# A hybrid attention and convolution layer on one core: last keys' product padded to 128 rows, Silu and Sqrt on ScalarE, a third seven-product pair in the first output block, halved first pieces and later copies

## The chip, the core and the metric

The kernel runs on one core of a Trainium2 chip. The core has five engines that run side by side and wait for each other through semaphores: TensorE (PE; its weight loads are shown as PEld), VectorE (DVE), ScalarE (ACT), GpSimd (POOL) and SyncE (SP), which issues most DMAs. The metric is the device time of one launch in microseconds (us), as a median of several runs. Each engine works its instructions in the order in which they were written to it, so an instruction that waits holds up what stands behind it on its engine.

## The reference

One layer over 272 positions (16 meta tokens ahead of 256 tokens), width 4096, all in float32. Only the 256 tokens' rows are returned.

```python
h = rmsnorm(x, norm_g)
p = h @ w_in                      # 4096 x 16384
q, k, v, g_attn, b, c, h, z = split(p)   # eight parts of 2048
o = stick_breaking_attention(q, k, v)    # 16 heads of 128, strictly causal
o = group_rmsnorm(o * silu(g_attn), attn_norm_g)
y = b * short_conv(c * h, conv_w)        # three taps along the positions
y = group_rmsnorm(y * silu(z), conv_norm_g)
return rmsnorm(x + concat([o, y]) @ w_out, final_norm_g)
```

## The kernel before

**Precision and products.** Each operand of a large product is split in a high part (a rounding cast on ACT, L409) and a low part (the rest, a subtraction on DVE, L405, called a "low" here). A product is then three products on TensorE: high by low, high by high, low by high (L442 to L444 for blocks, L450 to L453 for projections). Weights come in pieces of 128 x 1024, 512 KB each, through five buffers named `raw`; the split parts go to rings of six, `wh` and `wl`.

**Stages.** The sixteen heads and sixteen channel groups are worked as eight groups of two each. For a group the input projection has two kinds of pieces. Blocks ("p", one for each of k, v, c and h of a unit, four pieces of eight row chunks) give outputs with channels on the partitions; a piece is 24 products of 272 or 258 columns. Pairs (two row chunks, pieces "A" and "B") give q, g_attn, b and z with tokens on the partitions, 512 columns a product. A pair needs two by two token halves and column halves, eight products, three passes each. A **seven-product pair** does the same as Strassen's scheme does, in seven products, and has pieces "A", "B", "T", "U": sums of the tokens' blocks are made once and kept (`sum`, `lent`, in the output stage `osum`), sums of the weights are made on DVE at each pair (L426, L429, L431). Group 0 takes plain pairs only, the others seven-product pairs only.

Behind the eight groups comes the output projection: four blocks of 1024 (the last 768) columns, g = 8 to 11, in the same way over sixteen pairs each, and a last strip of 256 columns (pieces "o"). `sevens(g)` lists the pairs that take seven products: two (9, 10) in block 8, six (8 to 13) in the others. `OUT_ORDERS` gives the order of the pairs in each block. Behind a block's last seven-product pair `out_sums` (L921) adds its four special sums into the residual rows, eight DVE operations and one ACT copy; behind the block's last pair `out_blocks` (L972) evicts the four plain ones, eight DVE operations, and begins their squares. The sums of mixed pairs 8 to 13 (`kept_sums`, L302) are made when a group's mixed rows come back from memory (pieces "m" and "k").

**Order.** One loop over the pieces (L1026) writes everything: it loads seven pieces ahead, writes the products of piece i, splits piece i + 4, and then runs the tasks due at i (`later`, `run_tasks`). Up to the last pair of group 0, `top[0]`, and in the last eight pieces the order on the engines is left to the compiler's scheduler; between them it is the written order (`manual_schedule`, L1033).

**Attention of a group**, during the next group's pairs: queries are transposed, `scores` (L748) makes the masked scores, `weights` (L773) the weights through Abs, Tanh, Ln, Relu, two scans and Exp, `trans` (L794) turns them by 32 x 32 blocks into `at` (128 rows) and `a3` (the last sixteen keys, 16 rows). `v_block` (L586) does the same for the values, in `vv` (128 rows) and `v3` (16 rows); its copies are `vcopies` (L596). `po_mm` (L806) multiplies them: four products of 128 rows and one of 16 (L812). Then `squares`, `norm` and `mix` write the mixed rows. `plan_group` (L853) places all this; for the last group, 7, there is no next group, and it falls into the first output block, counted in pieces behind `f`, the end of the group's pairs.

**Gate.** `silu` (L668) computes Sigmoid on ACT and multiplies on POOL; the factor of the norm is put right later through `rt`, `rt2` and `fac`.

**Start.** TensorE runs ten products of a tile of ones (`warm`, L149) while x and the weights of the first pieces are loaded. `prep_x` scales x and splits it. The first two pieces are loaded and split in halves (`parts`, L371).

**Tail.** The last strip runs all products of tokens 0 to 127 first, then `finish(0)`, then those of tokens 128 to 255, then `finish(1)`. `finish` (L986) takes the inverse root by nine small DVE operations, a guess by integer arithmetic and two corrections, scales the rows in five parts on DVE and ACT and stores each.

## Time and profile before

| | before |
|---|---|
| runs | 1781.87, 1779.18, 1779.79 us |
| median | 1779.79 us |
| the profiled execution | 1778.96 us, its span 1777.2 us |
| TensorE clock granted | 0.998 |
| HBM read and written | 395.37 and 13.63 MB, 230 GB/s over the span |
| products (matmul instructions) | 10926 |
| first product of the kernel proper, last product | 6.87 us, 1765.51 us |

Times in the rows are counted from the first instruction of the span. A row of a timeline gives the start, the duration, engine, line, operation, what it writes and reads, shapes and how many were merged ("x2"); in square brackets the idle time of the engine before it and what ended it. A product's duration contains its passage through the array, and the next begins before it ends: the time that a product takes from TensorE's stream is read from start to start. A row of a group gives the count, the busy time, the mean of one in ns and idle time before. A row of waits names who waited for whom, the total in us, how often, and the longest.

### The profile page before, as it was taken

How to read it: one execution, taken by the hardware profiler on the slowest of the kernel's cores; microseconds unless marked ns; L12 is line 12 of the kernel's file. 1: busy time of each engine (PE TensorE's matmuls, PEld its weight loads, DVE VectorE, ACT ScalarE, POOL GpSimd, SP SyncE). 2: the span in 40 equal slices, each digit the busy share in tenths (PEclk: the TensorE clock that was granted, in tenths of full speed). 3: DMA queues.
4: the chain of work that ended last, by engine and by line, in shares of the span. 5: the costliest groups of instructions: out<-in, count | busy, mean ns of one | idle time of the engine just before them, and what ended most of it. 6: DMA issues, size and time to landing. Idle time of an engine off the chain costs nothing.

```text
span 1777.2 us, 29833 instructions
## 1 busy us (share of the span) xinstructions
PE 1762.1 (99%) x10926; PEld 1601.6 (90%) x10926; DVE 1590.3 (89%) x1929; ACT 1233.1 (69%) x2089; POOL 151.0 (8%) x184
## 2 busy tenths in 40 slices
PE   9999999999999999999999999999999999999997
PEld 7899999999999999999999999999999988888897
DVE  6776898999999999999999999999999888989986
ACT  6755677677767776777678768776777785555553
POOL 2143110011001100010101010101010110000000
PEclk9999999999999999999999999999999999999999
DMA  8977666766676667666766676667666676676565
GB/s 316 323 238 249 226 214 216 259 214 226 218 251 219 225 226 245 215 230 222 250 215 228 213 257 215 225 218 245 213 231 226 228 236 233 231 233 213 196 224 191
DMA packets 120819, 410.96 MB, mean 231 GB/s; under 512 B 13536, under 2 KB 18784, under 8 KB 120672
## 3 DMA queue, kind: packets, MB, share of 16 engines
q1 hardware_dynamic: 116640, 405.38, 67.3%
q10 hardware_dynamic: 4032, 3.67, 0.6%
q8 instruction: 86, 1.41, 0.3%
q14 instruction: 61, 0.50, 0.1%
HBM read 395.37 MB, written 13.63 MB: 230 GB/s over the span
## 4 chain that ended last, share of the span: by engine, by line
PE 97%; DMA 1%; ACT 1%; DVE 0%; SPq 0%; issue 0%; POOL 0%; DVEq 0%; ACTq 0%
PE P L450 17%; PE P L453 17%; PE P L452 17%; PE mm L444 14%; PE mm L443 14%; PE mm L442 14%; PE mo L955 0%; PE mo L954 0%; PE mo L953 0%; PE z L755 0%; PE po L812 0%; DMA mixd<-mfh 0%; ACT wh L409 0%; DMA raw<-w 0%; PE z L754 0%; DVE wl L405 0%
## 5 line engine op out<-in xcount | busy, mean ns | idle before, releaser
L405 DVE TENSOR_TENSOR wl<-raw,wh 128x1024 fp32r<-128x1024 f32 (+3 forms) x780 | 862.2, 1135 | 77.9 <-ACT wh L409 72.2
L409 ACT CAST wh<-raw 128x1024 fp32r<-128x1024 f32 (+3 forms) x780 | 721.0, 965 | 278.0 <-PE mm L443 68.2
L442 PE MATMUL mm<-xs,wh 128*128 128x258 f32 (+1 forms) x2048 | 582.5, 284 | 0.4 <-ACT wh L409 0.4
L444 PE MATMUL mm<-xs,wl 128*128 128x258 f32 (+1 forms) x2048 | 581.7, 284 | 0.8 <-DVE wl L405 0.8
L443 PE MATMUL mm<-xs,wh 128*128 128x258 f32 (+1 forms) x2048 | 581.7, 284 | 0.0
L442 PEld LDWEIGHTS mm<-xs,wh 128*128 128x128 f32 x2048 | 385.5, 188 | 4.6 <-ACT wh L409 0.8
L443 PEld LDWEIGHTS mm<-xs,wh 128*128 128x128 f32 x2048 | 385.7, 188 | 3.7
L444 PEld LDWEIGHTS mm<-xs,wl 128*128 128x128 f32 x2048 | 385.7, 188 | 1.0 <-DVE wl L405 1.0
L409 ACT CAST wh<-t 128x1024 fp32r<-128x1024 f32 (+1 forms) x132 | 137.7, 1043 | 142.9 <-DVE t L426 123.9
L450 PE MATMUL P<-wh,xs 128*128 128x512 f32 x464 | 180.8, 390 | 1.2 <-ACT wh L409 1.2
L453 PE MATMUL P<-wl,xs 128*128 128x512 f32 x464 | 180.7, 390 | 0.2 <-DVE wl L405 0.2
L452 PE MATMUL P<-wh,xs 128*128 128x512 f32 x464 | 180.5, 389 | 0.0
L405 DVE TENSOR_TENSOR wl<-t,wh 128x1024 fp32r<-128x1024 f32 (+1 forms) x132 | 158.7, 1202 | 8.8 <-ACT wh L409 8.8
L426 DVE TENSOR_TENSOR t<-raw,raw 128x1024 f32<-128x1024 f32 (+1 forms) x132 | 164.9, 1250 | 0.0
L450 PE MATMUL P<-wh,mixl 128*128 128x512 f32 (+1 forms) x412 | 155.7, 378 | 0.0
L453 PE MATMUL P<-wl,mixh 128*128 128x512 f32 (+1 forms) x412 | 155.1, 376 | 0.0
L452 PE MATMUL P<-wh,mixh 128*128 128x512 f32 (+1 forms) x412 | 155.0, 376 | 0.0
L450 PE MATMUL P<-wh,lent 128*128 128x512 f32 x308 | 123.6, 401 | 0.0
L453 PE MATMUL P<-wl,lent 128*128 128x512 f32 x308 | 120.2, 390 | 0.0
L452 PE MATMUL P<-wh,lent 128*128 128x512 f32 x308 | 120.1, 390 | 0.0
L450 PEld LDWEIGHTS P<-wh,xs 128*128 128x128 f32 x464 | 87.1, 188 | 19.8 <-ACT wh L409 1.4
L453 PEld LDWEIGHTS P<-wl,xs 128*128 128x128 f32 x464 | 87.1, 188 | 19.3 <-DVE wl L405 1.1
(238 smaller groups left out, 2136.5 us busy)
## 6 DMA issues: line engine op xcount, KB each, us to landing
raw<-w SPq DMA_DIRECT2D x614, 512.0 KB, 4.5
lent<-sumd SPq DMA_DIRECT2D x77, 512.0 KB, 5.9
raw<-w SPq DMA_DIRECT2D x32, 384.0 KB, 3.8
sumd<-lent SPq DMA_DIRECT2D x11, 512.0 KB, 5.2
raw<-xin SPq DMA_DIRECT2D x8, 512.0 KB, 5.4
raw<-mixd SPq DMA_DIRECT2D x8, 512.0 KB, 4.6
xr<-xt SPq DMA_DIRECT2D x15, 272.0 KB, 4.9
res<-xin SPq DMA_DIRECT2D x12, 256.0 KB, 4.9
```

The costliest lines, as they stand in the source:

```text
L405: nc.vector.tensor_tensor(out=lo[:, c], in0=t[:, c], in1=h[:, c].bitcast(F32), op=ALU.subtract)
L409: nc.scalar.copy(out=h[:, c], in_=t[:, c])
L426: nc.vector.tensor_tensor(out=s[:, :2 * hw].rearrange("p (a b) -> p a b", a=2), in0=a[:, :2 * hw].rearrange("p (a b) -> p a b", a=2), in1= ...
L442: nc.tensor.matmul(out=o, lhsT=h, rhs=x[:, 0, s:], start=k == 0, stop=False)
L443: nc.tensor.matmul(out=o, lhsT=h, rhs=x[:, 1, s:], start=False, stop=False)
L444: nc.tensor.matmul(out=o, lhsT=lo, rhs=x[:, 0, s:], start=False, stop=k == KC - 1)
L450: nc.tensor.matmul(out=o, lhsT=a[1], rhs=h, start=key not in begun, stop=False)
L452: nc.tensor.matmul(out=o, lhsT=a[0], rhs=h, start=False, stop=False)
L453: nc.tensor.matmul(out=o, lhsT=a[0], rhs=lo, start=False, stop=last)
```

## The change

- `a3` and `v3` get 128 rows, of which 16 are filled as before and the others stay zero; the two `v3` are made once and cleared on POOL at the start.
- The gate is one Silu on ACT in place; the tile `sg` and the products on POOL go, with them `rt2`.
- Pair 11 of block 8 takes seven products too. Block 9 is worked in the order 0 1 2 3 4 8 5 9 ... in place of 0 1 2 3 8 4 9 5 ....
- The values' transposes and copies of head 15 come two and three pieces behind the end of group 7's pairs, in place of its fourteenth pair (`v_block`), in a buffer of another ring; several tasks of the last group come one piece later.
- One warm-up product less; a one-column copy on ACT as its first work; five pieces instead of two split in halves; in the first two pieces the products with the high weights come ahead of those with the low ones, in twos; the cast of the kept token sums waits until the next piece "B" is split.
- The written order holds from the first piece on.
- `finish` takes Sqrt on ACT, a reciprocal and one correction on DVE.

```diff
-WARM = 10
+WARM = 9
+PARTS = 5
...
-    (0, 1, 2, 3, 8, 4, 9, 5, 10, 6, 11, 7, 12, 14, 13, 15),
+    (0, 1, 2, 3, 4, 8, 5, 9, 6, 10, 7, 11, 12, 14, 13, 15),
...
-    return OUT_SJ[1:3] if g == GROUPS else OUT_SJ if g > GROUPS else SJ if g else ()
+    return (9, 10, 11) if g == GROUPS else OUT_SJ if g > GROUPS else SJ if g else ()
...
     nc.vector.memset(ones, 1.0 / P)
+    first = wk.tile([P, P], F32, tag="junk", name="first")[:, :1]
+    nc.scalar.copy(out=first, in_=ones[:, :1])
...
-    a3 = const.tile([META, P], F32, name="a3")
+    a3 = const.tile([P, P], F32, name="a3")
     nc.vector.memset(a3, 0.0)
+    v3s = [const.tile([P, P], F32, name=f"v3{u}") for u in range(2)]
+    for u in range(2):
+        nc.gpsimd.memset(v3s[u], 0.0)
...
         f = raw_sums(t, j)
-        nc.scalar.copy(out=dst[:, 0], in_=f)
-        nc.vector.tensor_tensor(out=dst[:, 1], in0=f, in1=dst[:, 0].bitcast(F32), op=ALU.subtract)
+        def rest():
+            y = f
+            nc.scalar.copy(out=dst[:, 0], in_=y)
+            nc.vector.tensor_tensor(out=dst[:, 1], in0=y, in1=dst[:, 0].bitcast(F32), op=ALU.subtract)
+        held.append(rest)
...
-        parts = 2 if i < 2 else 1
+        parts = 2 if i < PARTS else 1
...
             c = slice(q * w // parts, (q + 1) * w // parts)
+            if i == 0:
+                prep_x(0, q)
             nc.scalar.copy(out=h[:, c], in_=t[:, c])
+            if i == 0 and q == 0:
+                nc.vector.tensor_scalar(out=xr[0][:, 1, :], in0=xr[0][:, 1, :], scalar1=pt[:, G0 + 1:G0 + 2], scalar2=None, op0=ALU.mult)
             if parts == 2:
                 low(c)
+        while held and p[0] == "B":
+            held.pop()()
...
+        if h is not None:
+            for q in (0, 1) if lo is None else (1, 0):
+                nc.tensor.matmul(out=o, lhsT=a[q], rhs=h, start=key not in begun, stop=False)
+                begun.add(key)
+        if lo is not None:
+            nc.tensor.matmul(out=o, lhsT=a[0], rhs=lo, start=False, stop=last)
+            left[key] -= 1
...
-            for i, k in enumerate((0, 1, 1, 1) if u < 2 else (0, 0, "p", 1) if u % 2 else (0, 0, "p", "p")):
+            for i, k in enumerate((0, 1, 1, 1) if u in (0, 1, 15) else (0, 0, "p", 1) if u % 2 else (0, 0, "p", "p")):
...
-            v3 = wk.tile([META, P], F32, tag=f"v3{u % 2}", name=f"v3{u}")
+            v3 = v3s[u % 2]
             for i in range(4):
-                A.copy(out=v3[:, 32 * i:32 * i + 32], in_=y[32 * i:32 * i + META, 2 * P:2 * P + 32])
+                A.copy(out=v3[:META, 32 * i:32 * i + 32], in_=y[32 * i:32 * i + META, 2 * P:2 * P + 32])
...
-                                    ((slot(g, 14, "p"), slot(g + 1, 1, "U")) if u < 15 else (slot(g, 13, "U"), slot(g, 14, "U"))) if u % 2 else
+                                    ((slot(g, 14, "p"), slot(g + 1, 1, "U")) if u < 15 else (after(fin[g], 2), after(fin[g], 3))) if u % 2 else
...
-        s = wk.tile([P, 2, 2, P], F32, tag="u2", name=f"sg{q}{g}", bufs=2)
         for t in range(2):
-            A.activation(out=s[:, t], in_=z[:, t], func=AF.Sigmoid, scale=rt[:, t:t + 1])
-            G.tensor_tensor(out=z[:, t], in0=z[:, t], in1=s[:, t], op=ALU.mult)
+            A.activation(out=z[:, t], in_=z[:, t], func=AF.Silu, scale=rt[:, t:t + 1])
...
-        later(after(f, 13), po, g, 0)
-        later(after(f, 13), trans, g, 1)
-        later(after(f, 17), po, g, 1)
+        later(after(f, 14), po, g, 0)
+        later(after(f, 14), trans, g, 1)
+        later(after(f, 18), po, g, 1)
         later(after(f, 17), squares, g, "c")
-        later(after(f, 19), squares, g, "h")
-        later(after(f, 20), norm, g)
-        later(after(f, 22), mix, g, "h")
-        later(after(f, 23), mix, g, "c")
+        later(after(f, 20), squares, g, "h")
+        later(after(f, 21), norm, g)
+        later(after(f, 23), mix, g, "h")
+        later(after(f, 24), mix, g, "c")
...
-        x, xb, y, ys, u = (const.tile([P, 1], F32, name=f"fin{t}_{i}") for i in range(5))
+        x, s, y, u = (const.tile([P, 1], F32, name=f"fin{t}_{i}") for i in range(4))
         v = nc.vector
+        nc.scalar.activation(out=s, in_=sqs[t], func=AF.Sqrt, scale=1.0 / D, bias=acc[t])
         v.scalar_tensor_tensor(out=x, in0=sqs[t], scalar=1.0 / D, in1=acc[t], op0=ALU.mult, op1=ALU.add)
-        v.tensor_scalar(out=y.bitcast(I32), in0=x.bitcast(I32), scalar1=-0.5, scalar2=SEED,
-                        op0=ALU.mult, op1=ALU.add)
-        v.tensor_scalar(out=xb, in0=x, scalar1=NB * NB, scalar2=None, op0=ALU.mult)
+        v.tensor_scalar(out=x, in0=x, scalar1=-0.5, scalar2=None, op0=ALU.mult)
+        v.reciprocal(out=y, in_=s)
         v.tensor_scalar(out=u, in0=y, scalar1=y, scalar2=x, op0=ALU.mult, op1=ALU.mult)
-        v.tensor_scalar(out=y, in0=u, scalar1=-NA, scalar2=y, op0=ALU.add, op1=ALU.mult)
-        v.tensor_scalar(out=u, in0=y, scalar1=y, scalar2=xb, op0=ALU.mult, op1=ALU.mult)
-        v.tensor_scalar(out=ys, in0=y, scalar1=RS, scalar2=None, op0=ALU.mult)
-        v.tensor_scalar(out=u, in0=u, scalar1=-10.0 / 3.0, scalar2=u, op0=ALU.add, op1=ALU.mult)
-        v.tensor_scalar(out=u, in0=u, scalar1=5.0, scalar2=ys, op0=ALU.add, op1=ALU.mult)
+        v.tensor_scalar(out=u, in0=u, scalar1=1.5, scalar2=y, op0=ALU.add, op1=ALU.mult)
...
-        if i == top[0] + 1:
+        if i == 1 - SPLITS:
             fixed = ExitStack()
             fixed.enter_context(tc.manual_schedule())
```

More of the change, by code (lines that the diff above doesn't have):

```diff
@@ L128 @@
     wp.tile([P, 56], F32, name="pad_w", bufs=1)
-    wk.tile([P, 46], F32, name="pad_wk")
+    wk.tile([P, 70], F32, name="pad_wk")
     pp = ctx.enter_context(tc.tile_pool(name="pp", bufs=1, space=bass.MemoryType.PSUM))
@@ L226 @@
     rq = const.tile([P, 2], F32, name="rq")
-    rt2 = const.tile([P, 2], F32, name="rt2")
     fac = const.tile([P, 8], F32, name="fac")
@@ L264, in load_x, with prep_x @@
         xr[j] = t
-    def prep_x(j, parts=1):
-        t = xr.pop(j)
+    def prep_x(j, c=None):
+        t = xr.pop(j) if c is None else xr[j]
         x = xs[j // 2][:, 2 * (j % 2):2 * (j % 2) + 2, :, :L]
-        for i in range(2):
+        for i in range(2) if c is None else (c,):
             g = pt[:, G0 + 2 * j + i:G0 + 2 * j + i + 1]
-            if i or parts == 2:
+            if c == 1:
+                pass
+            elif i and j > 2 or c == 0:
                 nc.vector.tensor_scalar(out=t[:, i, :], in0=t[:, i, :], scalar1=g, scalar2=None, op0=ALU.mult)
@@ L321, in token_sums @@
         f = raw_sums(t, j)
-        nc.scalar.copy(out=dst[:, 0], in_=f)
-        nc.vector.tensor_tensor(out=dst[:, 1], in0=f, in1=dst[:, 0].bitcast(F32), op=ALU.subtract)
+        def rest():
[3 more added lines that the diff above has]
+        held.append(rest)
+    held = []
     mixh, mixl = [], []
@@ L368, in split @@
         p = pieces[i]
-        if p[:2] == ("A", 0):
-            prep_x(p[2], 2 if p[2] == 0 else 1)
-        parts = 2 if i < 2 else 1
+        if p[:2] == ("A", 0) and i:
+            prep_x(p[2])
+        parts = 2 if i < PARTS else 1
         if p[0] == "x":
@@ L444, in mm_k, with mm_p @@
         nc.tensor.matmul(out=o, lhsT=lo, rhs=x[:, 0, s:], start=False, stop=k == KC - 1)
-    def mm_p(key, j, a, h, lo):
+    def mm_p(key, a, h, lo):
         o = psum[key][:, :hwid(key[0])]
         last = left[key] == 1
-        nc.tensor.matmul(out=o, lhsT=a[1], rhs=h, start=key not in begun, stop=False)
-        begun.add(key)
-        nc.tensor.matmul(out=o, lhsT=a[0], rhs=h, start=False, stop=False)
-        nc.tensor.matmul(out=o, lhsT=a[0], rhs=lo, start=False, stop=last)
-        left[key] -= 1
+        if h is not None:
[5 more added lines that the diff above has]
+            left[key] -= 1
     begun, left = set(), {}
@@ L502, in mm_in @@
                 psum[key] = bank(f"P{q}_{p[1]}", (q + 4 * p[1]) % 8)
-            mm_p(key, p[2], st, wh[:, c], wl[:, c])
+            if i < 2:
+                mm_p(key, st, wh[:, c], None)
+                lows_.append((key, st, None, wl[:, c]))
+                if len(lows_) < 2:
+                    continue
+                for t in lows_:
+                    mm_p(*t)
+                lows_.clear()
+            else:
+                mm_p(key, st, wh[:, c], wl[:, c])
     def block_bank(i):
@@ L564, in finish_stats @@
         V.tensor_scalar(out=rq, in0=rt, scalar1=1.0 / math.sqrt(P), scalar2=None, op0=ALU.mult)
-        V.tensor_tensor(out=rt2, in0=rt, in1=rt, op=ALU.mult)
-        for q in range(4):
-            V.tensor_scalar(out=fac[:, 2 * q:2 * q + 2], in0=rt if q < 2 else rt2, scalar1=RS, scalar2=None,
-                            op0=ALU.mult)
+        V.memset(fac[:, :4], RS)
+        for q in range(2, 4):
+            V.tensor_scalar(out=fac[:, 2 * q:2 * q + 2], in0=rt, scalar1=RS, scalar2=None, op0=ALU.mult)
     def blocks(dst, src, n, i, engines):
@@ L591, in vtrans @@
         def vtrans():
-            y = wk.tile([P, 416], F32, tag="zs", name=f"yv{u}")
+            y = (wk.tile([P, 512], F32, tag="u2", name=f"yv{u}", bufs=2) if u == 15 else
+                 wk.tile([P, 416], F32, tag="zs", name=f"yv{u}"))
             V.transpose(out=y[:, :L + META], in_=vt[:, :L + META])
@@ L803, in trans @@
         A.copy(out=at[:META, P - META:P], in_=y[96:96 + META, 400:416])
-        A.copy(out=a3[:, P - META:], in_=y[96:96 + META, 432:448])
+        A.copy(out=a3[:META, P - META:], in_=y[96:96 + META, 432:448])
     def po_mm(g, u, o):
@@ L1065 @@
             g = p[1]
-            if p[0] == "U" and p[2] == sevens(g)[-1]:
+            if p[0] == "U" and p[2] == [j for j in OUT_ORDERS[g - GROUPS] if seven(g, j)][-1]:
                 later(i + 1, out_sums, g)
-            for q, j in enumerate((9, 14) if g == GROUPS else (10, 6)):
+            for q, j in enumerate((9, 14) if g == GROUPS else (10, 6) if g > GROUPS + 1 else (OUT_ORDERS[1][8], OUT_ORDERS[1][9])):
                 if p[0] == "B" and p[2] == j:
```

13 lines of the change are left out of this document (7 added, 6 removed).

## The prediction, made before the changed kernel was run

> **What bounds the kernel now.** First the page: its top two lines and the chain that ended last. Then the waits of TensorE alone.
>
> ```profile
> span 1777.2 us, 29833 instructions
> ...
> PE 1762.1 (99%) x10926; PEld 1601.6 (90%) x10926; DVE 1590.3 (89%) x1929; ACT 1233.1 (69%) x2089; POOL 151.0 (8%) x184
> ...
> PE 97%; DMA 1%; ACT 1%; DVE 0%; SPq 0%; issue 0%; POOL 0%; DVEq 0%; ACTq 0%
> ```
>
> ```profile
> PE mm L444 <- DVE wl L405: 0.8, 1, 0.8
> PE mm L442 <- ACT wh L409: 0.4, 1, 0.4
> ```
>
> The chain lies on TensorE for 97% of the span, and behind the opening TensorE waits at one place only (0.8 + 0.4). So a microsecond is gained by making TensorE's own stream shorter, by these few waits, or in the stretches before its first and behind its last product. What DVE, ACT and POOL save is worth nothing of itself; what they are given costs nothing until it comes later than TensorE.
>
> **The padded product.** The timeline of TensorE around one attention output (`po`); a row of "x2" is one product in two passes.
>
> ```profile
> 257.18 0.39 PE L810 MATMUL po<-vv,at 128*128 128x128 f32 x2
> 257.40 0.39 PE L811 MATMUL po<-vv,at 128*128 128x128 f32 x2
> 257.72 0.48 PE L812 MATMUL po<-v,a 16*128 16x128 f32 x2
> 258.13 0.50 PE L450 MATMUL P<-wh,lent 128*128 128x512 f32 x1
> 258.47 0.39 PE L452 MATMUL P<-wh,lent 128*128 128x512 f32 x1
> 258.70 0.40 PE L453 MATMUL P<-wl,lent 128*128 128x512 f32 x1
> ```
>
> ```profile
> L812 PE MATMUL po<-v,a x32: 270/321/372, 257.7 to 1460.9; 16*128 16x128 f32 x32
> ```
>
> Read the starts, not the durations. A product of 128 rows takes 257.40 − 257.18 = 0.22 us, a projection product of 512 columns 258.70 − 258.47 = 0.23. From the start of L811 to that of L452 pass 1.07 us, where 0.22 + 0.22 + 0.23 = 0.67 would do if the 16-row product ran like its neighbours. So each `po` loses 0.40 us, before, in and behind the one product that uses 16 rows. The second row has 32 passes of it, 16 outputs, all of that form. Padding `a3` and `v3` to 128 rows makes it the form of L811: 16 × 0.40 = **6.4 us** less, all on TensorE. No instruction is added but memsets in the first microseconds; the copies that fill the two tiles stay.
>
> A rule speaks against this. The Trainium skill, "TensorE: Matmul & The Clock Gate", section "Why this matters for your kernels", says that a single product of 32 rows takes as long as one of 128, the gain of few rows being concurrency. By it padding is worth nothing and the sum is smaller by this term (the first rival). The rows differ, though: 0.41 against 0.22 us from start to start. The skill's "TensorEngine Tiling (Array Packing)", section "Key Properties", says that a change of tiling mode drains TensorE; by that page the loss on both sides of L812 goes with the padding.
>
> **The late copies.** TensorE's one wait in mid-kernel, and a group of ACT's from 1393 us to 1401.3 us.
>
> ```profile
> 1401.36 0.39 PE L453 MATMUL P<-wl,lent 128*128 128x512 f32 x1
> ...
> 1403.63 0.28 PE L442 MATMUL mm<-xs,wh 128*128 128x258 f32 x1
> 1403.75 0.28 PE L443 MATMUL mm<-xs,wh 128*128 128x258 f32 x1
> ```
>
> ```profile
> L576 ACT COPY vv<-yv 32x64 f32<-32x64 f32 x16 | 3.9, 243 | 0.2
> ```
>
> From 1401.36 to 1403.63 pass 2.27 us for one projection product (0.23) and three block products (0.12 each, the last two rows), 0.59 in all: 1.7 us lost. The weights' cast was late because ACT first did sixteen small copies of the last head's values, 3.9 us, and four smaller ones. The change puts all of them behind the group's last seven-product pairs, four a piece. The casts then come up to 3.9 us sooner or more, and DVE, which followed ACT, is next: it was through with the piece before about when TensorE was, so I leave 0.2 us of wait. I take **−1.5 us**; bounds 0 and −1.7.
>
> In their new place the copies need ACT's time between the scores and their weights.
>
> ```profile
> 1423.34 1.24 ACT L765 ACTIVATE zl<-zm 128x416 f32<-128x416 f32 x2 [2.52 <-DVE zm L763]
> ```
>
> There ACT stands idle for 2.52 us until the masked scores come; about three of the five portions fall ahead of that, two behind it, so that the chain to `po` comes some 2 us later. The change moves both `po`, the transposes, squares, norm and `mix` of the last group one piece later, 12 products, 2.7 us, and covers it. If the cover is gone, TensorE waits in `po` of the last group: up to 1 us.
>
> **The third seven-product pair.** Pair 11 of the first output block takes 7 × 3 instead of 8 × 3 products of 512 columns: 3 × 0.23 = **0.7 us** less. Its sums exist already (block 1 uses them). DVE pays. Its lead at this pair (the last of the four lows is that of the pair's first piece, the row under it TensorE's first product with that piece), then two groups of its operations:
>
> ```profile
> 1492.43 4.63 DVE L405 TENSOR_TENSOR wl<-raw,wh 128x1024 fp32r<-128x1024 f32 x4
> ```
>
> ```profile
> 1501.64 0.39 PE L450 MATMUL P<-wh,mixl 128*128 128x512 f32 x1
> ```
>
> ```profile
> L405 DVE TENSOR_TENSOR wl<-raw,wh 128x1024 fp32r<-128x1024 f32 x612 | 733.4, 1234 | 70.1 <-ACT wh L409 65.6
> L426 DVE TENSOR_TENSOR t<-raw,raw 128x1024 f32<-128x1024 f32 x126 | 159.2, 1264 | 0.0
> ```
>
> A plain pair costs DVE two lows, 2.5 us; a seven-product pair three lows of 1.23, one sum of 1.26 and three operations of half the width, some 0.7 each: 7.1. So 4.6 us more. And `out_sums`, eight operations of about 0.7, now falls two pieces ahead of the block's eviction (eight more) instead of six. DVE's lead is 1501.6 − 1497.1 = 4.5 us where the pair begins. From there to the fifth piece of the next block TensorE works 21 × 0.23 + 6 × 2.7 = 21 us, DVE 7.1 + 7 × 1.2 + 16 × 0.7 = 26.7, one low of which, 1.2, is counted in the lead: 25.5. So the lead is just used up there. The reordered second block puts its first seven-product pair one pair later, which gives 2 × (2.7 − 1.2) = 3 us before more sums fall due. Cost nothing, bounds 0 and +2.
>
> **The start.** ACT, DVE, SP and TensorE; the last row is the issue of that first half weight tile, with the time to its landing.
>
> ```profile
> 3.90 1.28 ACT L276 ACT_TABLE_LOAD   x1 [3.90 <-DMA xr<-xt]
> ...
> 6.20 1.66 ACT L409 CAST wh<-raw 128x512 fp32r<-128x512 f32 x3
> ```
>
> ```profile
> 3.94 0.36 DVE L272 TENSOR_SCALAR xr<-xr,pt 128x272 f32<-128x272 f32 x1 [2.15 <-DMA xr<-xt]
> ```
>
> ```profile
> 6.87 0.50 PE L450 MATMUL P<-wh,xs 128*128 128x512 f32 x1 [1.23 <-ACT wh L409]
> ```
>
> ```profile
> 1.71 0.42 SPq L358 DMA_DIRECT2D raw<-w  x1
> ```
>
> ```profile
> raw<-w SPq DMA_DIRECT2D x1, 256.0 KB, 3.2
> ```
>
> Now the first ACT work waits for x and then loads its table, 1.28 us. A copy of one column right behind the first memset draws the load to the first microseconds, where ACT has nothing. Then: scaled x at 4.30, its cast (half as wide as one of 0.55) to 4.7, half tile landed at 1.71 + 3.2 = 4.9, cast (1.66 for three, 0.55 each) to about 5.5, and the first product, which now takes the high halves of x and weights alone, at about 5.6 instead of 6.87. One warm-up product less frees TensorE sooner. Halving five pieces instead of two and holding the token sums back keeps the casts short and in line; the later landings of weights stay, so I take **−1.2 us**, bounds −0.3 and −1.5. Up to 95 us the work now runs in the written order; I put 0.4 us of new waits to this and to block 0 together.
>
> **The tail.** DVE after the last product.
>
> ```profile
> 1766.83 0.16 DVE L989 SCALAR_TENSOR_TENSOR fin<-sq,acc 128x1 f32<-128x1 f32 x1
> ...
> 1767.21 0.27 DVE L993 TENSOR_SCALAR fin<-fin,fin 128x1 f32<-128x1 f32 x1
> 1767.52 0.21 DVE L994 TENSOR_SCALAR fin<-fin,fin 128x1 f32<-128x1 f32 x1
> ...
> 1768.58 1.81 DVE L1003 TENSOR_SCALAR res<-res,fin 128x256 f32<-128x256 f32 x3
> ```
>
> Nine small operations take 1768.58 − 1766.83 = 1.75 us. ACT's nearest operation is a narrow Exp:
>
> ```profile
> L790 ACT ACTIVATE za<-zs 128x16 f32<-128x16 f32 x16 | 3.2, 200 | 0.0
> ```
>
> After: Sqrt on ACT, which no row shows, between 0.2 by this row and the 0.55 of a 512-column cast; I take 0.3, nearer to the narrow one. Two DVE steps run beside it, then come reciprocal 0.2 and two steps like L993 (0.31 to the next start): 1.1. **−0.65 us**, bounds −0.3 and −0.9. Sqrt's table load, 1.28, falls to the first half of the tokens, under TensorE's last products; DVE's reciprocal waits for it there, and queued behind that are the scalings of the first half alone, whose stores have until the second half's begin.
>
> **Nothing** for Silu (ACT runs as many activations, POOL loses its products, and neither is on the chain) and the dropped `rt2`. If Silu and Tanh shared no table, each group would have one load more, 1.28 us on an engine that is 69% busy.
>
> **Sum**: 6.4 + 1.5 + 0.7 + 1.2 + 0.65 − 0.4 = 10.0 us. The profiled run took 1778.96 (1777.2 and 1.8 around it), so 1769.0; the median of the three runs is 0.8 above it, so **1769.8 us**.
>
> **The rivals.** (1) Padding gains nothing, because the 0.40 us belong to the order of tiles and not to the rows: −3.6, 1776.2. Against it: the neighbours of the same output. 5%. (It is the first of the skill's rules above.) (2) The waits come back: DVE is late behind pair 11 (+2), ACT in the last `po` (+1), and the stall at 1402 stays (+1.5): 1774.3. For it DVE's lead, used up. 8%. (3) Slower: the opening in written order.
>
> ```profile
> ACT sum L322 <- POOL sf L317: 8.5, 5, 2.0
> ```
>
> ```profile
> 60.00:70.00 10.00, 10.00 (x46) 8.29 (x45) 8.69 (x20) 9.00 (x13) 0.00 (x0) 1.00 0.82 288
> ```
>
> (Behind the stretch's length stand the busy times of PE, weight loads, DVE, ACT and POOL.) ACT has 1.0 us free in these 10, 0.55 per pair of 5.45 us. It can wait on POOL for 1.7 us at a time, as the first row shows. If an in-order wait costs ACT more than 0.55 us in every pair, the opening runs at ACT's pace; slower overall by 0.2% it is from 13.6 us, 0.85 a pair: 1783.4. Against it: the waits for POOL are those that are held back. 3%. (4) The change does only its arithmetic, start and tail unchanged: 1769.8 + 1.2 + 0.65 = 1771.6, 10%. The forecast: 74%.
>
> The range, 1767.5 to 1775, takes in (2), (4) and the bounds. Within 0.2%, 3.6 us, is what a measurement of this kernel can tell from no change: faster 93%, same 4%, slower 3%.
>
> **What would show it.** L812 as 128*128 at 0.22 us a pair of passes; no wait of TensorE near 1400; 24 products in pair 11 become 21; the first product near 5.6; the last scaling 1.1 us behind the last square. It is wrong if TensorE shows new waits above 1 us in the opening or near 1500.

## The result, and the profile after

The changed kernel took **1770.24 us** (median of 6 runs, 1769.37 to 1770.37), the kernel before, beside it, 1779.66 us (1777.83 to 1781.87). The ratio is 0.9946, 95% interval 0.9933 to 0.9959: faster by about half a per cent. The prediction was 1769.8 us in a range of 1767.5 to 1775. The profiled run took 1770.3 us, 1768.6 of it span.

First the page of the changed kernel (its head, the busy times, the chain by engine) and, of its waits, TensorE's.

```profile
span 1768.6 us, 29794 instructions
...
PE 1755.4 (99%) x10921; PEld 1598.1 (90%) x10921; DVE 1578.7 (89%) x1925; ACT 1233.9 (70%) x2100; POOL 113.2 (6%) x154
...
PE 99%; DMA 0%; DVE 0%; SPq 0%; ACT 0%; issue 0%; DVEq 0%; ACTq 0%
```

```profile
PE warm L152 <- DVE ones L147: 1.1, 1, 1.1
PE P L471 <- DVE xs L287: 0.7, 1, 0.7
PE P L474 <- DVE wl L418: 0.3, 1, 0.3
PE P L471 <- ACT wh L424: 0.2, 1, 0.2
```

The chain is TensorE's for 99% of the span instead of 97%, and the two waits of mid-kernel (0.8 and 0.4) are off the list. All on this list lie in the opening; one more, of 0.43 us, shows on the weight loads alone and comes below. TensorE has five entries less: the three products of pair 11 and the two passes of one warming product.

Since TensorE sets the end, the gain is read best as a running account: when does the same product start in both traces? The table takes the first product of a piece; the numbers are starts in the two timelines.

| first product of | before, us | after, us | gained so far |
|---|---|---|---|
| piece 0 | 6.87 | 5.58 | 1.29 |
| third pair | 18.71 | 18.47 | 0.24 |
| `T` piece of pair 11, group 1 (two outputs `po` later) | 291.48 | 290.51 | 0.97 |
| `T` piece of pair 14, group 5 | 1020.54 | 1016.64 | 3.90 |
| `U` piece of pair 15, group 5 | 1048.77 | 1045.31 | 3.46 |
| block of head 15, kind 2, fourth part | 1406.13 | 1399.58 | 6.55 |
| pair 5 of output block 2 | 1637.24 | 1629.25 | 7.99 |
| (last scaling of the second tokens) | 1768.58 | 1759.91 | 8.67 |

The steps between these rows are the terms of the prediction. The padding shows as a step of 0.36 or 0.37 us at each of the sixteen outputs, 14 of them ahead of the row of head 15 and two behind it: 16 × 0.365 = 5.8. The start gives 1.29 and loses 1.05 of it again within 13 us. In group 5 there is a loss of 0.44 that the prediction did not look for there. The stall of 1402 us gives 1.68, pair 11 0.68, the tail 0.67. Together 0.24 + 5.84 − 0.44 + 1.68 + 0.68 + 0.67 = 8.67, where the spans differ by 8.6. (In the medians it is 9.4, since the profiled run of before, 1778.96, lay under its own median.)

The padded product, in the changed kernel's timeline of TensorE:

```profile
257.16 0.39 PE L840 MATMUL po<-vv,at 128*128 128x128 f32 x2
257.38 0.39 PE L841 MATMUL po<-v,a 128*128 128x128 f32 x2
257.53 0.71 PE L471 MATMUL P<-wh,lent 128*128 128x512 f32 x2
```

From L840 to the projection product behind L841 pass 257.53 − 257.16 = 0.37 us. Before, from L811 to L450, they were 258.13 − 257.40 = 0.73.

The tail, DVE and then ACT:

```profile
1758.83 0.16 DVE L1019 SCALAR_TENSOR_TENSOR fin<-sq,acc 128x1 f32<-128x1 f32 x1
...
1759.15 0.17 DVE L1021 RECIPROCAL fin<-fin 128x1 f32<-128x1 f32 x1
...
1759.91 1.81 DVE L1028 TENSOR_SCALAR res<-res,fin 128x256 f32<-128x256 f32 x3
```

```profile
1758.83 0.29 ACT L1018 ACTIVATE fin<-sq,acc 128x1 f32<-128x1 f32 x1
```

From the first small operation to the first scaling pass 1759.91 − 1758.83 = 1.08 us, before 1.75. The root took 0.29 us, and two DVE steps run beside it.

The opening, TensorE's rows (a row of "x4" is four products in the new order, high halves first):

```profile
5.58 1.20 PE L471 MATMUL P<-wh,xs 128*128 128x512 f32 x4 [0.25 <-ACT wh L424]
7.07 0.74 PE L474 MATMUL P<-wl,xs 128*128 128x512 f32 x2 [0.30 <-DVE wl L418]
...
12.57 0.70 PE L471 MATMUL P<-wh,xs 128*128 128x512 f32 x2 [0.67 <-DVE xs L287]
```

The first product comes at 5.58 us, as predicted (5.6). But then TensorE waits for low halves at 7.07, and at 12.57 for the x of the second pair. At that product the whole gain is gone: before, it started at 12.46. ACT shows what that x, landed at 9.85, still has to go through, two scalings and a cast, before VectorE makes its low half:

```profile
9.93 0.94 ACT L281 ACTIVATE xr<-xr,pt 128x272 f32<-128x272 f32 x2 [0.19 <-DMA raw<-w]
10.90 0.65 ACT L286 CAST xs<-xr 128x544 fp32r<-128x544 f32 x1
```

### The profile page after: what moved, and what is told of

It reads as the page before. It is cut to its first block, busy times and chain, and to the rows that moved or that the text cites. A ratio compares the mean times of both kernels' runs of the same rounds, so it can differ in the third digit from the quotient of the medians.

```text
span 1768.6 us, 29794 instructions
## 1 busy us (share of the span) xinstructions
PE 1755.4 (99%) x10921; PEld 1598.1 (90%) x10921; DVE 1578.7 (89%) x1925; ACT 1233.9 (70%) x2100; POOL 113.2 (6%) x154
## 4 chain that ended last, share of the span: by engine, by line
PE 99%; DMA 0%; DVE 0%; SPq 0%; ACT 0%; issue 0%; DVEq 0%; ACTq 0%
PE P L471 35%; PE P L474 18%; PE mm L462 14%; PE mm L461 14%; PE mm L463 14%; PE mo L984 0%; PE mo L983 0%; PE mo L982 0%; PE z L784 0%; DMA xr<-xt 0%; PE z L783 0%; PE po L838 0%; PE po L841 0%; PE po L840 0%; PE po L839 0%; PE po L837 0%
## 5 line engine op out<-in xcount | busy, mean ns | idle before, releaser
L418 DVE TENSOR_TENSOR wl<-raw,wh 128x1024 fp32r<-128x1024 f32 (+2 forms) x784 | 857.1, 1124 | 71.4 <-ACT wh L424 65.8
L424 ACT CAST wh<-raw 128x1024 fp32r<-128x1024 f32 (+2 forms) x784 | 720.3, 961 | 254.4 <-DVE raw L450 57.9
L471 PE MATMUL P<-wh,xs 128*128 128x512 f32 x928 | 285.6, 390 | 0.9 <-DVE xs L287 0.7
L471 PEld LDWEIGHTS P<-wh,xs 128*128 128x128 f32 x928 | 174.1, 188 | 38.2 <-ACT wh L424 1.6
L471 PE MATMUL P<-wh,lent 128*128 128x512 f32 x616 | 193.5, 395 | 0.0
L471 PEld LDWEIGHTS P<-wh,lent 128*128 128x128 f32 x616 | 109.5, 188 | 17.2
L450 DVE TENSOR_TENSOR raw<-raw 128x512 f32<-128x512 f32 (+1 forms) x133 | 92.2, 693 | 4.6
```

What stands on the lines that cost most here:

```text
L418: nc.vector.tensor_tensor(out=lo[:, c], in0=t[:, c], in1=h[:, c].bitcast(F32), op=ALU.subtract)
L424: nc.scalar.copy(out=h[:, c], in_=t[:, c])
L450: nc.vector.tensor_tensor(out=t[:, c1], in0=t[:, c1], in1=t[:, c2], op=ALU.add)
L471: nc.tensor.matmul(out=o, lhsT=a[q], rhs=h, start=key not in begun, stop=False)
```

## The experiments

Three questions were open: whether the 0.36 us per output belong to the rows; why the start gave back four fifths of its gain; and where the 0.44 us in group 5 come from. A fourth came up on the way.

**Rows of the last keys' product.** One kernel gives every group another number of rows.

```diff
-        T.matmul(out=o[:, P:SEQ], lhsT=a3, rhs=v3, start=False, stop=True)
+        T.matmul(out=o[:, P:SEQ], lhsT=a3[:ROWS[g]], rhs=v3[:ROWS[g]], start=False, stop=True)
+    ROWS = (128, 16, 32, 64, 96, 128, 64, 16)
```

> The changed kernel, with the last key product of group g reading only the first 128, 16, 32, 64, 96, 128, 64, 16 rows (g = 0 to 7) of the same zero-padded tiles; the sums are the same. In the changed kernel each padded product put the rest of the kernel 0.36 us earlier. Theory A, any product of fewer than 128 rows breaks the stream of 128-row products at one price: both products of groups 1, 2, 3, 4, 6 and 7 lose 0.36 us each whatever their rows, groups 0 and 5 nothing, in all +4.4 us (about 1774.6). Theory B, the price goes with the missing rows: about 0.36 at 16, 0.31 at 32, 0.21 at 64, 0.10 at 96, in all +3.1 us (about 1773.3). Theory C, rows cost nothing and the steps of 0.36 us came from something else beside these products: no group differs, 1770.

It took 1772.98 us (one run). TensorE's rows in the groups with 16, 64 and 96 rows, from the last 128-row product of the output on (those with 32 rows, at 607.32, 607.64 and 608.05 us, lie as the ones with 16 do):

```profile
431.58 0.39 PE L842 MATMUL po<-vv,at 128*128 128x128 f32 x2
431.90 0.48 PE L843 MATMUL po<-v,a 16*128 16x128 f32 x2
432.31 0.73 PE L471 MATMUL P<-wh,lent 128*128 128x512 f32 x2
...
783.05 0.39 PE L842 MATMUL po<-vv,at 128*128 128x128 f32 x2
783.37 0.48 PE L843 MATMUL po<-v,a 64*128 64x128 f32 x2
783.79 0.73 PE L471 MATMUL P<-wh,lent 128*128 128x512 f32 x2
...
958.83 0.39 PE L842 MATMUL po<-vv,at 128*128 128x128 f32 x2
959.06 0.39 PE L843 MATMUL po<-v,a 96*128 96x128 f32 x2
959.20 0.71 PE L471 MATMUL P<-wh,lent 128*128 128x512 f32 x2
```

From L842 to the projection product it is 0.73, 0.73, 0.74 and 0.37 us for 16, 32, 64 and 96 rows. So neither theory A nor theory B holds as it was put: the price is one and the same at 16, 32 and 64 rows, and nothing at 96. It doesn't go with the missing rows; it has two values. The rows are shown to be the cause; how TensorE loses the time is not. The Trainium skill, "TensorEngine Tiling (Array Packing)", section "Available Configurations", knows row tiles of 32, 64 and 128, and its section "Key Properties" says that a change of tiling mode drains the engine. That would fit every value, if a product of 64 rows or fewer runs in a row tile and one of 96 in the full array; no run here shows the mode itself. By this trace padding to 96 rows would have done as well as to 128.

**The late copies.** The copies of the last head's values go back to their old place, the rest of the change stays.

```diff
-   (after(fin[g], 2), after(fin[g], 3))
+   (slot(g, 13, "U"), slot(g, 14, "U"))
```

(the part of the line that changes; also the old spacing and buffer of these copies)

> The changed kernel with the transposition and the copies of the last head's values back at their old places (slots 13 and 14 of the last group, old spacing of the copies, old tile). Theory A, these copies in front of the block casts on ScalarE were the wait of 1402 us: a wait of 1.4 to 1.8 us in the blocks behind the last group, near 1397 us, and about +1.6 us on the time (1771.9). Theory B, it was Silu and the taken-out multiplications that gave ScalarE its lead there: no wait above 0.3 us, time within 0.4 us of the changed kernel.

It took 1771.41 us (5 runs, 1769.91 to 1771.59). TensorE's rows, and ACT's ahead of them:

```profile
1395.97 0.39 PE L474 MATMUL P<-wl,lent 128*128 128x512 f32 x1
1396.79 0.39 PE L461 MATMUL mm<-xs,wh 128*128 128x258 f32 x1 [0.43 <-ACT wh L424]
...
1398.05 0.39 PE L463 MATMUL mm<-xs,wl 128*128 128x258 f32 x1 [0.76 <-DVE wl L418]
1398.27 0.28 PE L461 MATMUL mm<-xs,wh 128*128 128x258 f32 x1
```

```profile
1392.68 1.05 ACT L424 CAST wh<-raw 128x1024 fp32r<-128x1024 f32 x1
1393.76 1.00 ACT L606 COPY vv<-yv 32x64 f32<-32x64 f32 x4
```

The stall is back in its old form, first the cast, then the low half: 1398.27 − 1395.97 = 2.30 us for 0.59 us of products, 1.7 us. Theory A holds: Silu and the rest are the same here, and the stall is back. One more thing differs, though. Just ahead of these casts ACT waits for a store of mixed rows to land: 1.97 us in the kernel before, 2.01 in this one, but 0.45 in the trace of the changed kernel. The second run of the changed kernel (after_again, below) settles it: there ACT waited 2.13 us at that place, without the copies, and from there to 1410 us TensorE kept step with the first trace. So the late store alone makes no stall; whether the copies alone would, no trace shows. The spans differ by less, 1769.7 against 1768.6, since this execution hadn't the 0.44 us of group 5.

**The start: scalings and order.** Two edits that should bring the second pair's x sooner.

```diff
-            elif i and j > 2 or c == 0:
+            elif i or c == 0:
...
-            if i == 0 and q == 0:
-                nc.vector.tensor_scalar(out=xr[0][:, 1, :], in0=xr[0][:, 1, :], scalar1=pt[:, G0 + 1:G0 + 2], scalar2=None, op0=ALU.mult)
             if parts == 2:
                 low(c)
+            if i == 0 and q == 0:
+                nc.vector.tensor_scalar(out=xr[0][:, 1, :], in0=xr[0][:, 1, :], scalar1=pt[:, G0 + 1:G0 + 2], scalar2=None, op0=ALU.mult)
```

> The changed kernel with two edits in the opening: VectorE makes the first low half of piece 0 before it scales the second half of x, and for pairs 1 and 2 the second scaling of x goes to VectorE as it did before the change. Theory A, what the earlier first product gains is lost at the second pair, whose x lands at 9.85 us and is then scaled twice on ScalarE: the second pair's first product comes at 11.8 to 12.1 instead of 12.57, the third pair's at 17.4 to 17.9 instead of 18.47, and the time falls by 0.5 to 1.0 us. Theory B, the landings alone decide (weights of the second pair at 11.11, x of the third at 13.04): both come within 0.2 us of the changed kernel's, and so does the time.

It took 1770.72 us (1770.08 to 1771.07). The second pair began at 13.75 us and the third at 19.19, both later than in the changed kernel: neither theory. The first copy taken out shows the same, only more.

```diff
-    first = wk.tile([P, P], F32, tag="junk", name="first")[:, :1]
-    nc.scalar.copy(out=first, in_=ones[:, :1])
```

> The changed kernel without the one-column copy ahead of the warming products, so that ScalarE's first table load comes with its first cast. Theory A, the start is capped by the second pair: the first product moves from 5.58 to about 6.4 us, but the third pair still starts within 0.3 us of 18.47 and the time is within 0.4 us. Theory B, the prediction's sum, the start passes through: the third pair starts 0.7 to 1.1 us later and the time rises by as much (1771.1).

1770.91 us (1769.35 to 1771.79), third pair at 19.86, 1.39 later than in the changed kernel. Theory B seems to have it, but not by a start that is passed on: in both traces the first eight to ten products start 0.43 us apart, where the changed kernel's took 0.23. So the next question was TensorE's clock, and the changed kernel itself was run again, beside kernels with more and with less warming.

> The changed kernel once more, beside the next three. Theory A, the opening is a matter of TensorE's clock, which stands at half until TensorE has been busy for a while, and of when in its own time the clock looks: passes of 128 columns start 0.21 us apart when cold and 0.11 when warm, so the first 24 products either run at 0.23 us as in the profile of the changed kernel, or at 0.43 up to about 10.5 us as in the two looks before; then the third pair starts 0.7 to 1.4 us later than 18.47. One more draw of that, and a median within 0.5 us of 1770.2. Theory B, those two slow openings came from their edits: the first products run at 0.23 us here.

1770.62 us (1769.56 to 1771.52). The same program as in the section above, another execution; TensorE's rows:

```profile
5.96 2.08 PE L471 MATMUL P<-wh,xs 128*128 128x512 f32 x4 [0.63 <-ACT wh L424]
7.83 1.05 PE L474 MATMUL P<-wl,xs 128*128 128x512 f32 x2
...
10.90 1.09 PE L471 MATMUL P<-wh,xs 128*128 128x512 f32 x4
11.83 0.62 PE L474 MATMUL P<-wl,xs 128*128 128x512 f32 x2
```

Four products take 7.83 − 5.96 = 1.87 us up to 8 us; from 10.90 on four start in 11.83 − 10.90 = 0.93. One program, two openings: theory A. The slow one brought the third pair to 19.10. The view by stretches shows why no clock column would have told it (behind the length of the stretch 6 to 10 us stand PE, weight loads, DVE, ACT, POOL, then the granted clock):

```profile
6.00:10.00 4.00, 4.00 (x10) 3.13 (x11) 2.77 (x6) 2.48 (x5) 0.00 (x0) 1.00 0.96 341
```

Ten products in 4 us, where the changed kernel's first trace has seventeen, and yet a granted clock of 1.00 in both: that column doesn't show this slowness. The Trainium skill, "TensorE: Matmul & The Clock Gate", section "What's actually happening", says that TensorE runs at half clock until it has been busy for one window of about 3.4 us, that the windows run freely, and that an idle one closes the gate again. The runs agree: half speed or full and nothing between, and the same program's opening falls to one side or the other. The idle time ahead of the first product doesn't decide it by itself: 0.25 us in the first trace and 0.63 in this one, but 1.35 in the run late_back, whose products were fast.

```diff
-WARM = 9
+WARM = 11
```

> The changed kernel with 11 warming products instead of 9, so that TensorE is busy (at half clock to about 5.97 us) until the first product's data are there. Theory A (the clock falls to, or stays at, half over the idle gap between the warming and the first product): no slow product behind about 7.5 us, the third pair starts at 18.5 or before, and the median is 0.2 to 0.7 us under that of the changed kernel beside it. Theory B (the gap has no part): slow openings as often as with 9, or a first product only pushed later; median within 0.2 us.

1769.6 us (1769.22 to 1770.03), 1.0 below the changed kernel beside it. The trace has four products in 1.04 us from the first on, and the third pair at 18.29:

```profile
1.12 4.14 PE L152 MATMUL warm<-ones 128*128 128x128 f32 x22 [1.12 <-DVE ones L147]
5.79 1.20 PE L471 MATMUL P<-wh,xs 128*128 128x512 f32 x4 [0.54 <-ACT wh L424]
6.83 0.69 PE L474 MATMUL P<-wl,xs 128*128 128x512 f32 x2
```

Those are the signs of theory A, with a median further down than its 0.2 to 0.7. But eleven products did not close the idle gap, as it supposed: their 22 passes took 4.14 us, where 18 took 4.21 in the changed kernel, and the gap is 0.54 us. TensorE was at full speed before the warming ended, and the gap did no harm.

The counter-test warms with three products only:

> The changed kernel with 3 warming products, which end near 2.5 us, so that TensorE is idle for over 3 us ahead of the first product. Theory A (clock): in every execution the first products start 0.43 us apart until some 3 to 4 us of work are done; the second piece starts at 10.9 to 11.9 instead of 9.02, the third pair 0.6 to 1.5 us later than 18.47; median 0.3 to 1.3 us over that of the changed kernel, and 1.0 to 2.0 over that with 11 warming products. Theory B (no such clock): first products 0.23 us apart, third pair within 0.3 us.

1770.53 us (1769.91 to 1771.29), first products 0.43 us apart until 12.2 us, third pair at 19.96, 1.67 later than with eleven.

```profile
6.14 2.07 PE L471 MATMUL P<-wh,xs 128*128 128x512 f32 x4 [3.37 <-ACT wh L424]
```

That is theory A for the opening. In spans it is 1769.6 against 1768.2 with eleven, in medians 0.9 us. The kernels with three and with eleven were run in different rounds. Each against the kernel before of its own round, three warming products gain 8.7 us, eleven 9.9, and the changed kernel 9.4 and 8.9 in its two rounds. That is the order theory A asks for, but differences of this size lie within the intervals of the ratios, so the times alone don't show it.

With the clock out of the way the two edits of the opening could be tried again:

> 11 warming products and the two edits of the run open_split (low half of piece 0 ahead of the second scaling of x, second scalings of pairs 1 and 2 on VectorE). Theory A, open_split lost only by its cold products: the second pair's first product comes about 0.5 us earlier than in the run with 11 warming products alone, and the third pair's 0.3 to 0.9 us earlier; median 0.3 to 0.9 us lower than there. Theory B, the landings decide: third pair within 0.2 us of that run's.

1769.85 us (1769.5 to 1770.28); second pair at 12.40, third at 18.31, within 0.02 of the run with eleven warming products alone. By its sign that is theory B, the landings decide. But the edit hardly shortened the way of x: VectorE was still at a low half when it should have scaled, ACT waited 0.37 us for it, and the cast of x began at 10.73 us in both. So this run doesn't tell whether a shorter way of x would help; the landings in the other traces are the better evidence. Where the first products ran at full speed (in same_place all but three) the third pair starts a fixed time behind the landing of the second pair's x:

| kernel | x of the second pair landed, us | third pair, us | between |
|---|---|---|---|
| before | 9.29 | 18.71 | 9.42 |
| changed kernel | 9.85 | 18.47 | 8.62 |
| rows_by_group | 9.26 | 17.89 | 8.63 |
| late_back | 9.82 | 18.44 | 8.62 |
| warm11 | 9.68 | 18.29 | 8.61 |
| warm11_open | 9.74 | 18.31 | 8.57 |
| same_place (below) | 10.37 | 19.00 | 8.63 |

Whether the first product came at 5.58 or at 6.11 doesn't matter. What does is the landing, which moves by over 1 us between the executions, and what follows it: 8.6 us in all six with the change, 9.42 in the one trace of before.

**The stores and the root.** The second stored mixes get buffers of their own, and the last factor is the reciprocal of the root alone.

```diff
-   m = wk.tile([P, SEQ], F32, tag="u2", name=f"mf{q}{g}_{u}", bufs=2)
+   m = (wk.tile([P, SEQ], F32, tag="u2", name=f"mf{q}{g}_{u}", bufs=2) if q == "h" else
+        wk.tile([P, 448], F32, tag=f"zl{i}", name=f"mf{q}{g}_{u}")[:, :SEQ])
...
-        v.reciprocal(out=y, in_=s)
-        v.tensor_scalar(out=u, in0=y, scalar1=y, scalar2=x, op0=ALU.mult, op1=ALU.mult)
-        v.tensor_scalar(out=u, in0=u, scalar1=1.5, scalar2=y, op0=ALU.add, op1=ALU.mult)
+        v.reciprocal(out=u, in_=s)
```

> The changed kernel with two edits that lie far apart. The second pair of stored mixes gets buffers of its own, so that ScalarE doesn't wait for the first pair's store: expected, no wait of ScalarE for a landing at the c mixes (it was 2.18 us in group 5, whose T piece of pair 15 made TensorE wait 0.44 us), TensorE's wait there gone, 0 to 0.5 us by how the stores land. And the last factor is the reciprocal of ScalarE's root alone, without the refining step on VectorE (the result keeps the root's own accuracy): the last scaling 0.55 us earlier behind the last square than 1.08 us. Rival for the tail: the scaling starts no earlier because the stores' issue holds it. Median 0.5 to 1.0 us under the changed kernel beside it.

It took **1789.11 us** (1788.71 to 1790.12), 18.5 more than the changed kernel beside it. Yet ACT's wait for the stores, of which the changed kernel has seven, is not among its waits any more:

```profile
ACT mfc L754 <- DMA mixd<-mfh: 6.0, 7, 2.2
```

The edits did what they were to do, and the kernel became slower all along. The loss has no one place: each group is about 2 us longer. The row of the last keys' product, from the first output to the last, in the changed kernel and in this one:

```profile
L841 PE MATMUL po<-v,a x32: 275/275/275, 257.4 to 1456.5; 128*128 128x128 f32 x32
```

```profile
L842 PE MATMUL po<-v,a x32: 275/275/275, 261.9 to 1474.2; 128*128 128x128 f32 x32
```

1199.1 us against 1212.3 for the same products. Measured from start to start, projection products of 512 columns lie 227 ns apart in the one (median) and 230 to 231 in the other. TensorE's granted clock is 0.997 and 0.998, and in the slower one its list of waits has nothing behind the opening. The edit had dropped four one-column tiles. By the addresses in the built programs, which no view of a profile shows, all weight tiles and sums lay 128 bytes lower in each partition for it, while x lay where it was. Two kernels separate the cause:

```diff
-    wk.tile([P, 70], F32, name="pad_wk")
+    wk.tile([P, 102], F32, name="pad_wk")
```

(same_place: the two edits again, with the old bytes; also eleven warming products, and pieces 2 and 3 taking x's high half first)

> The two edits of store_root (own buffers for the second stored mixes, last factor without the refining step), 11 warming products, and pieces 2 and 3 of the opening taking the high half of x first; and the padding tile of the work pool 32 floats longer, so that weights and sums lie at the same bytes as in the changed kernel (store_root had four one-column tiles less and lay 128 bytes lower). Theory A, the 19 us of store_root were the place of its operands in memory: projection products start 227 ns apart again (median; 230 to 231 there), and the time is that of the changed kernel less 1 to 2.2 us (warming 0.5 to 1.0, second pair 0.3 to 0.5, stores 0 to 0.5, tail 0.5): 1768.0 to 1769.3. Theory B, it was one of the two edits: 1786 to 1789 again.

```diff
-    wk.tile([P, 70], F32, name="pad_wk")
+    wk.tile([P, 46], F32, name="pad_wk")
```

(shift96: the changed kernel and nothing else)

> The changed kernel with the padding tile of the work pool back at 46 floats, as in the kernel before: weights and sums lie 96 bytes lower than in either kernel, x stays. Theory A, TensorE's rate goes with the distance of its two operands in memory: every product's pitch changes by a few ns, and the time by +5 to +25 us (128 bytes lower cost 19). Theory B, a shift of 128 bytes is special or the 19 us came from elsewhere: within 1 us of the changed kernel.

same_place took 1769.36 us (1768.99 to 1769.77), shift96 **1791.68 us** (1791.39 to 1792.53; ratio to before 1.0071, interval 1.0056 to 1.0086). The row of shift96:

```profile
L841 PE MATMUL po<-v,a x32: 275/275/275, 262.3 to 1476.0; 128*128 128x128 f32 x32
```

1213.7 us. In same_place projection products lie 227 ns apart again, in shift96 231. Theory A in both (same_place lies 0.06 us above its range): the rate of TensorE hangs on where its operands lie, and 96 bytes are worth over twice the whole change. So the change has one more line, which its list and its diff above don't show: it lengthens this tile, `pad_wk`, from 46 to 70 floats. The dropped `rt2` and two `fin` tiles would have moved all weights by 96 bytes, and with the 24 floats they lie at the bytes of before. The tile moves everything behind it, weights, sums and the tiles of the other engines. Whether the distance between weights and x counts, or the weights' own place, is not separated, and why these places are better was not tried.

In same_place the new order of pieces 2 and 3 gained nothing (second pair at 12.64, its x having landed at 10.37, the latest of all). The tail is shorter by what was expected. ACT's square, then DVE's reciprocal and scaling:

```profile
1758.33 0.39 ACT L996 ACTIVATE junk<-y 128x256 f32<-128x256 f32 x1 [5.53 <-DVE y L991]
```

```profile
1759.20 0.16 DVE L1020 RECIPROCAL fin<-fin 128x1 f32<-128x1 f32 x1 [0.44 <-ACT fin L1019]
1759.40 1.81 DVE L1025 TENSOR_SCALAR res<-res,fin 128x256 f32<-128x256 f32 x3
```

From the square to the scaling pass 1.07 us, against 1759.91 − 1758.29 = 1.62 in the changed kernel: 0.55 less.

The stores are the other edit. In the changed kernel the loss of group 5 shows on ACT and on the weight loads:

```profile
1035.21 0.48 ACT L754 ACTIVATE mfc<-mxc,pt 128x256 f32<-128x256 f32 x1 [2.18 <-DMA mixd<-mfh]
```

```profile
1044.26 0.19 PEld L474 LDWEIGHTS P<-wl,lent 128*128 128x128 f32 x1 [0.43 <-DVE wl L418]
```

ACT waits 2.18 us for a store to land before it may fill its buffer again; the casts, the sums of pair 15 and the low half follow late, and TensorE waits 0.43 us. The second of those stores took 5.84 us to land. In rows_by_group, late_back and no_first, with the same code there, it took 4.05 to 5.16 us, and the weight loads waited for nothing; in after_again, open_split and warm11_open it took 5.49 to 5.82, and they waited 0.2 to 0.5 us. The loss comes and goes with the landing. In same_place the store took 4.03 us, so the lack of a loss there proves nothing for the buffers; the last kernel is their test.

**The x of the second pair ahead.** The last kernel follows the table above: that x is loaded ahead of the second half of piece 1.

```diff
                 if i == 0 and h == 0:
                     nc.sync.dma_start(out=xr[0][:, 1:, :], in_=xt[:, 1:2, :])
+                if i == 1 and h == 0:
+                    load_x(1)
...
+            if i == 1 and q == 1:
+                prep_x(1)
...
```

(this x is no longer loaded and prepared at its old place, and its second scaling is on VectorE; with the edits of store_root at the old bytes and eleven warming products)

> The two edits of store_root with weights and sums at the changed kernel's bytes, 11 warming products, and the x of the second pair loaded ahead of the second half of piece 1 and prepared ahead of that half's cast, its second scaling on VectorE. In the looks so far with a warm opening the third pair began 8.6 us behind the landing of the second pair's x, whenever that came (9.26 to 10.37). Theory A, that landing sets the start: x lands near 9.0, the second pair's first product comes at 11.9 to 12.2, the third pair at 17.4 to 17.8 (18.47 in the changed kernel); with the tail 0.5 and the stores 0 to 0.5 the median is 1768.0 to 1768.9. Theory B, the half of piece 1 that now lands and is cast later takes its place: the third pair at 18.1 to 18.6, median 1769.0 to 1769.6.

It took **1769.17 us** (1768.54 to 1770.17; ratio to before 0.9944, interval 0.9931 to 0.9958), span 1767.4. The x landed at 8.83, a microsecond sooner, and the third pair began at 18.38. Theory B: the wait has only moved, to the second half of piece 1.

```profile
11.09 1.19 PE L475 MATMUL P<-wh,xs 128*128 128x512 f32 x4 [0.61 <-ACT wh L428]
```

It also tests the stores' buffers: the second store of group 5 took 5.83 us to land, as long as in the changed kernel, but ACT's next mix no longer waits for it,

```profile
1033.35 0.48 ACT L759 ACTIVATE mfc<-mxc,pt 128x256 f32<-128x256 f32 x1 [0.40 <-ACT mfc L759]
```

and TensorE's weight loads have no wait there.

It is the fastest of all by its median, 1.1 us under the 1770.24 of the changed kernel. Between the two traces, with spans of 1767.4 and 1768.6, 0.1 us comes from the opening, 0.5 from group 5 and the rest from the tail. Differences of this size are within the intervals of the ratios; the trace carries them, not the times. Its last factor keeps the root's own accuracy.

## Why the prediction was right, and where it was not

The sum was −10.0 us on the profiled run; the profiles give −8.7, the medians −9.4.

- **Padding, −6.4: right in kind, too large by 0.6.** The term of 0.40 per output counted from L811 to the second projection product and took 0.67 us for what would be left. The changed kernel needs 0.68 there, a gain of 0.39; but ten products further on about 0.365 is left of it, and that is what the account keeps at each output. So the term was read too near to the product. The first rival (the rows cost nothing) is refuted, and with it, for a product that stands among 128-row ones, the rule of the Trainium skill on which it stood ("TensorE: Matmul & The Clock Gate", section "Why this matters for your kernels"): 16 rows took 0.36 us more than 128.
- **Late copies, −1.5: 1.7.** The 0.2 us left for a DVE that would be late next were not needed.
- **Third seven-product pair, −0.7: 0.68.** DVE's lead, by the prediction "just used up", was enough: no wait of TensorE there, and the second rival did not come.
- **Start, −1.2: 0.24 in the profiled pair. This is the step that failed.** The first product came at 5.58 as worked out, but the step let the gain pass through. The prediction wrote "the later landings of weights stay" and then did not ask which of them is next: it is the x of the second pair. Before the change it was ready at 11.63 us, only 0.8 ahead of the second pair's first product, while TensorE worked without a break from its first product up to there:

```profile
10.90 0.73 DVE L280 TENSOR_TENSOR xs<-xr,xs 128x544 fp32r<-128x544 f32 x1 [0.77 <-ACT xs L279]
```

```profile
12.46 0.39 PE L450 MATMUL P<-wh,xs 128*128 128x512 f32 x1
```

In the changed kernel it was ready at 12.43, and TensorE waited. Of these 0.80 us, 0.56 are the later landing of this execution, and 0.24 the change's own doing: ACT now makes both scalings of that x, where DVE made one. So nothing of the 1.29 us reached the second pair (12.46 before, 12.57 after); what is left at the third pair comes from inside the second, which took 6.25 us before and 5.90 after: TensorE waited twice for low halves there, 0.2 and 0.3 us, and now only once. Had x landed as in the one trace of before, the opening would have gained 9.42 − 8.62 = 0.8 us, an estimate. And "one warm-up product less frees TensorE sooner" was taken for a help. The second run of the changed kernel had a slow opening, and its third pair came at 19.10, 9.39 behind the landing instead of 8.62. Of the eight traces with nine warming products three had the first eight to ten products slow (after_again, open_split, no_first); of the four with eleven none had more than three (same_place). Whether ten would have done was not tried.
- **New waits, +0.4: 0.44, but elsewhere, and that the numbers agree is luck.** It lies at the store in group 5 and goes with that store's landing. The opening's own new waits are in the start's term, and the first output block shows none.
- **Tail, −0.65: 0.67**, the root 0.29 for 0.3. Sqrt's table load came where it was put, in the first half's finish:

```profile
1750.12 1.28 ACT L1018 ACT_TABLE_LOAD   x1
1751.41 0.29 ACT L1018 ACTIVATE fin<-sq,acc 128x1 f32<-128x1 f32 x1
```

- **Nothing for Silu: right.** The third rival (an opening at ACT's pace) did not come: from the third pair to the first `po`, at 257 us, the account stays at 0.24.

The prediction took the rate of TensorE's products as given, and that held only by an edit that it did not name: without the longer padding tile the same change (shift96) is slower than the kernel before by 0.7%.

## What to carry to other kernels

Where one engine sets the end, keep a running account of the same instruction's start in both traces: it puts each gain and each loss in its place, also those that only one execution has. A gain at the start passes on only as far as the next transfer and the work on it have slack, so ask for every one of the first few which is next. And when tiles are added or dropped, look where the operands of the bounding engine come to lie before you judge the edit by its time.

## What the runs showed of the hardware

- Shifting the weights and sums, with the rest of their pool, by 96 or 128 bytes while x stayed cost some 21 and 18.5 us, 1% of the kernel: 1213.7 and 1212.3 us from the first output to the last instead of 1199.1, with the same products between.
- A product of 16, 32 or 64 rows between products of 128 cost 0.36 us more than one of 128, each the same; one of 96 rows cost nothing more.
- TensorE's first products ran 0.43 or 0.23 us apart in two executions of the same program, with a granted clock of 1.00 in both.
- The landing of one transfer in the opening, issued at 4.07 us each time, varied from 9.26 to 10.37 us between executions with the same loads ahead of it.
